# GpSimd's maximum over partitions: `partition_all_reduce` against the stock `tensor_reduce` into one partition

## Chip, cores, metric

One core of one Trainium2 chip. The metric is the device time of one execution in microseconds (us). The profile is of one execution; its span is shorter than the reported time (164.46 against 162.6 for the kernel before).

## The reference

```python
def setup_inputs():
    batch, seq, dim = 32, 512, 1024
    return {"x": np.random.randn(batch, seq, dim).astype(np.float32)}

def reference(x):
    return np.max(x, axis=-1).astype(np.float32)
```

This is 16,384 rows of 1024 f32, 67.1 MB in, one maximum per row out. A block of 128 rows is one row per partition, so there are 128 blocks.

## The kernel before

The rows are loaded into a ring of 46 blocks, and VectorE takes the row maxima (`reduce` below). Five of the 128 blocks, all from loads near the end, go by a side road, so that VectorE has less to do there. On it TensorE turns a block, after which a row's 1024 values lie over 128 partitions and 8 chunks; ScalarE copies it out of PSUM; GpSimd takes the maximum over the partitions; TensorE turns the one row of answers back; VectorE merges the 8 chunks.

```python
TENSOR = {                      # after which load which block is turned or turned back
    8: [("turn", 8, 0), ("back", 8, 0)],
    9: [("turn", 9, 0), ("turn", 9, 1), ("turn", 9, 2), ("back", 9, 0)],
    12: [("turn", 12, 0), ("back", 9, 1), ("back", 9, 2), ("back", 12, 0)],
}
BY_GPSIMD = {8: 1, 9: 3, 12: 1} # blocks of each load that take the side road
MERGE = {9: 8, 15: 9, 18: 12}   # after which load VectorE merges whose blocks
# ... cut ...
    turned = ctx.enter_context(tc.tile_pool(name="turned", bufs=2))
    allr = ctx.enter_context(tc.tile_pool(name="allr", bufs=2))
# ... cut ...
    def turn(j, k):
        rows, cols = tiles[j]
        ps = psum.tile([P, D], F32)
        for c in range(C):
            in_turn("PE", nc.tensor.transpose(out=ps[:, c * P:(c + 1) * P],
                in_=rows[:, k, c * P:(c + 1) * P], identity=ident))
        sb = turned.tile([P, D], F32)
        nc.scalar.copy(out=sb, in_=ps)
        top = allr.tile([P, D], F32)
        nc.gpsimd.partition_all_reduce(top, sb, P, bass_isa.ReduceOp.max)
        tops[j, k] = top

    def back(j, k):
        # ... cut ...
        for c in range(C):
            in_turn("PE", nc.tensor.transpose(out=backs[j][:, k, c:c + 1],
                in_=tops[j, k][0:1, c * P:(c + 1) * P], identity=ident[0:1, 0:1]))
# ... cut: for each load
            reduce = in_turn("DVE", nc.vector.reduce_max(
                out=cols[:, :n - m], in_=xc[:, :n - m, :], axis=X))
            if j in MERGE:
                i = MERGE[j]
                in_turn("DVE", nc.vector.reduce_max(out=tiles[i][1], in_=backs[i], axis=X))
```

VectorE and TensorE run in program order. A merge that isn't ready therefore stops VectorE.

## Time and profile before

| | before |
|---|---|
| time | 164.46 us (2 runs, 164.42 to 164.5) |
| VectorE busy | 135.0 us, 83% of the span |
| GpSimd busy | 16.3 us, 10% |
| loads' share of the DMA engines | 96.6% |

Two things are nearly full, VectorE at the end and the DMA engines throughout. GpSimd is idle for its first 134 us.

### The profile page before, as it was taken

What the parts mean: (1) busy time and instruction counts of PE and PEld (TensorE: products, weight loads), DVE (VectorE), ACT (ScalarE), POOL (GpSimd) and SP (SyncE); (2) the same over time, 40 slices, a digit from 0 to 9 for tenths busy, and PEclk for the clock granted to TensorE, in tenths of its full rate; (3) what the DMA queues carried; (4) which work ended last, traced back from release to release, by engine and by line L of the source; (5) the groups of instructions that cost most, each with busy time, mean ns of one, the idle gap of its engine ahead of it and who ended that gap; (6) DMA issues with size and microseconds to landing.
All of it is one profiled execution on the core that took longest, in us unless ns stands there. A gap on an engine that the chain in (4) does not pass through costs nothing.

```text
span 162.6 us, 293 instructions
## 1 busy us (share of the span) xinstructions
PE 13.0 (8%) x80; PEld 11.7 (7%) x80; DVE 135.0 (83%) x33; ACT 6.3 (4%) x6; POOL 16.3 (10%) x9
## 2 busy tenths in 40 slices
PE   0000000000000000000000000000000040943520
PEld 0000000000000000000000000000000030933420
DVE  3000079995999779999996999999999999999994
ACT  3000000000000000000000000000000011240200
POOL 0000000000000000000000000000000007099910
PEclk9999999999999999999999999999999999985555
DMA  7999699988999799999998989999999999999990
GB/s 242 484 484 438 287 484 484 484 378 348 484 484 484 333 498 432 445 419 419 419 419 387 499 388 427 417 426 408 417 435 435 471 399 426 423 418 409 406 368 16
DMA packets 3456, 67.18 MB, mean 413 GB/s; under 512 B 640, under 2 KB 640, under 8 KB 1792
## 3 DMA queue, kind: packets, MB, share of 16 engines
q1 hardware_dynamic: 3168, 67.11, 96.6%
q10 hardware_dynamic: 288, 0.07, 0.2%
HBM read 67.11 MB, written 0.07 MB: 413 GB/s over the span
## 4 chain that ended last, share of the span: by engine, by line
DVE 54%; DMA 44%; SPq 0%; issue 0%
DVE res L139 53%; DMA ring<-in_x_dram 44%; DVE res L156 0%; DVE tail L155 0%; SPq L133 0%; DVE res L143 0%
## 5 line engine op out<-in xcount | busy, mean ns | idle before, releaser
L139 DVE TENSOR_REDUCE res<-ring 128x1 f32<-128x1024 f32 (+6 forms) x20 | 132.1, 6653 | 24.3 <-DMA ring<-in_x_dram 24.3
L106 POOL PARTITION_ALL_REDUCE top<-sb x5 | 16.1, 3255 | 138.8 <-ACT sb L104 138.8
L98 PE MATMUL ps<-ident,ring 128*128 128x128 f32 x40 | 8.1, 382 | 134.2 <-DMA ring<-in_x_dram 131.8
L98 PEld LDWEIGHTS ps<-ident,ring 128*128 128x128 f32 x40 | 7.1, 204 | 134.3 <-issue 134.2
L104 ACT COPY sb<-ps 128x1024 f32<-128x1024 f32 x5 | 5.1, 1013 | 144.9 <-PE ps L98 143.0
L115 PE MATMUL fetched<-ident,top 1*128 1x1 f32 x40 | 5.0, 243 | 9.1 <-POOL top L106 9.1
L115 PEld LDWEIGHTS fetched<-ident,top 1*128 1x128 f32 x40 | 4.6, 214 | 10.3 <-POOL top L106 9.8
L104 ACT ACT_TABLE_LOAD x1 | 1.3, 1283 | 0.7 <-PEq L176 0.7
L76 DVE MEMSET ident<- 128x128 f32 x1 | 0.2, 165 | 0.8 <-PEq L176 0.8
L156 DVE TENSOR_REDUCE res<-tail 128x1 f32<-128x513 f32 x1 | 0.7, 686 | 0.0
L155 DVE TENSOR_REDUCE tail<-ring 128x1 f32<-128x512 f32 x1 | 0.7, 675 | 0.0
L83 DVE TENSOR_SCALAR rowno<-rowno 32x1 f32<-32x1 f32 x3 | 0.4, 147 | 0.1
L143 DVE TENSOR_REDUCE res<-fetched 128x1 f32<-128x8 f32 (+1 forms) x3 | 0.5, 161 | 0.0
L78 DVE TENSOR_TENSOR_SCAN colno<-ident 128x128 f32<-128x128 f32 x1 | 0.4, 425 | 0.0
L85 DVE TENSOR_SCALAR ident<-colno,rowno 128x128 f32<-128x128 f32 x1 | 0.3, 287 | 0.0
L80 DVE STREAM_TRANSPOSE rowno<-colno 128x32 f32<-128x32 f32 x1 | 0.2, 211 | 0.0
L176 POOL MEMSET const-float32-0.0<- 128x1 f32 x1 | 0.1, 99 | 0.2 <-issue 0.2
L176 POOL MEMSET const-uint8-127<- 128x1 uint8 x1 | 0.1, 103 | 0.0
L176 POOL MEMSET const-bfloat16-1.0<- 128x1 bf16 x1 | 0.1, 102 | 0.0
L176 POOL MEMSET const-float32-1.0<- 128x1 f32 x1 | 0.1, 99 | 0.0
L77 DVE MEMSET rowno<- 128x32 f32 x1 | 0.1, 85 | 0.0
## 6 DMA issues: line engine op xcount, KB each, us to landing
ring<-in_x_dram SPq DMA_DIRECT2D x3, 7680.0 KB, 38.4
ring<-in_x_dram SPq DMA_DIRECT2D x2, 6656.0 KB, 34.6
ring<-in_x_dram SPq DMA_DIRECT2D x2, 4608.0 KB, 37.8
ring<-in_x_dram SPq DMA_DIRECT2D x2, 3072.0 KB, 31.9
ring<-in_x_dram SPq DMA_DIRECT2D x1, 5632.0 KB, 28.6
ring<-in_x_dram SPq DMA_DIRECT2D x7, 512.0 KB, 22.3
ring<-in_x_dram SPq DMA_DIRECT2D x2, 1536.0 KB, 34.9
ring<-in_x_dram SPq DMA_DIRECT2D x1, 1024.0 KB, 33.4
```

The costliest lines, as they stand in the source:

```text
L78: in_turn("DVE", nc.vector.tensor_tensor_scan(out=colno, data0=ident, data1=ident, initial=-1.0, op0=ALU.add, op1=ALU.mult))
L83: in_turn("DVE", nc.vector.tensor_scalar(out=part, in0=part, scalar1=float(q * 32), scalar2=None, op0=ALU.add))
L85: in_turn("DVE", nc.vector.tensor_scalar(out=ident, in0=colno, scalar1=rowno[:, 0:1], scalar2=None, op0=ALU.is_equal))
L98: in_turn("PE", nc.tensor.transpose(out=ps[:, c * P:(c + 1) * P], in_=rows[:, k, c * P:(c + 1) * P], identity=ident,))
L104: nc.scalar.copy(out=sb, in_=ps)
L106: nc.gpsimd.partition_all_reduce(top, sb, P, bass_isa.ReduceOp.max)
L115: in_turn("PE", nc.tensor.transpose(out=backs[j][:, k, c:c + 1], in_=tops[j, k][0:1, c * P:(c + 1) * P], identity=ident[0:1, 0:1],))
L139: reduce = in_turn("DVE", nc.vector.reduce_max(out=cols[:, :n - m], in_=xc[:, :n - m, :], axis=X))
L143: in_turn("DVE", nc.vector.reduce_max(out=tiles[i][1], in_=backs[i], axis=X))
L155: in_turn("DVE", nc.vector.reduce_max(out=tail[:, PAD - 1:PAD], in_=half, axis=X))
L156: in_turn("DVE", nc.vector.reduce_max(out=res[:, I - 1:], in_=tail[:, PAD - 1:], axis=X))
L176: nc = _bacc.Bacc("TRN2", target_bir_lowering=False, num_devices=1)
```

## The change

The intent is to use the stock instruction: a `tensor_reduce` over the partition axis needs no special routine and writes one partition, which is all that `back` reads, where `partition_all_reduce` writes the answer to all 128.

```diff
-from concourse import bass_isa, bass_utils, mybir
+from concourse import bass_utils, mybir
@@
-        top = allr.tile([P, D], F32)
-        nc.gpsimd.partition_all_reduce(top, sb, P, bass_isa.ReduceOp.max)
+        top = allr.tile([1, D], F32)
+        nc.gpsimd.tensor_reduce(out=top, in_=sb, axis=mybir.AxisListType.C, op=ALU.max)
```

## The prediction

> **What bounds the kernel now.** I read the chain of work that ended last first, because only what lies on it can move the end.
>
> ```profile
> DVE 54%; DMA 44%; SPq 0%; issue 0%
> DVE res L139 53%; DMA ring<-in_x_dram 44%; DVE res L156 0%; DVE tail L155 0%; SPq L133 0%; DVE res L143 0%
> ```
>
> GpSimd (POOL) is not on it. The span of 162.6 us is loads followed by VectorE's row maxima (L139), and at the end VectorE alone. Then the groups of instructions, for what GpSimd does and how long each takes:
>
> ```profile
> L139 DVE TENSOR_REDUCE res<-ring 128x1 f32<-128x1024 f32 (+6 forms) x20 | 132.1, 6653 | 24.3 <-DMA ring<-in_x_dram 24.3
> L106 POOL PARTITION_ALL_REDUCE top<-sb x5 | 16.1, 3255 | 138.8 <-ACT sb L104 138.8
> L104 ACT COPY sb<-ps 128x1024 f32<-128x1024 f32 x5 | 5.1, 1013 | 144.9 <-PE ps L98 143.0
> L115 PE MATMUL fetched<-ident,top 1*128 1x1 f32 x40 | 5.0, 243 | 9.1 <-POOL top L106 9.1
> L143 DVE TENSOR_REDUCE res<-fetched 128x1 f32<-128x8 f32 (+1 forms) x3 | 0.5, 161 | 0.0
> ```
>
> Five blocks of 128 rows leave VectorE: TensorE turns each (L98), ScalarE copies it out (L104), GpSimd takes the maximum over the 128 partitions in 3.255 us (L106), TensorE turns the answer back from partition 0 (L115), and VectorE merges it (L143). The last column of L143 is an idle time of 0.0: VectorE never waits for this side road. Its slack comes from the timeline near the end, whose columns are start, length, engine and operation:
>
> ```profile
> 133.73 1.01 ACT L104 COPY sb<-ps 128x1024 f32<-128x1024 f32 x1 [131.73 <-PE ps L98]
> 134.84 3.23 POOL L106 PARTITION_ALL_REDUCE top<-sb  x1 [134.41 <-ACT sb L104]
> 138.11 1.01 PE L115 MATMUL fetched<-ident,top 1*128 1x1 f32 x8 [4.42 <-POOL top L106]
> 142.17 9.64 POOL L106 PARTITION_ALL_REDUCE top<-sb  x3 [4.11 <-ACT sb L104]
> 142.93 0.15 DVE L143 TENSOR_REDUCE res<-fetched 128x1 f32<-128x8 f32 x1
> 150.80 2.07 PE L115 MATMUL fetched<-ident,top 1*128 1x1 f32 x16
> 152.06 3.23 POOL L106 PARTITION_ALL_REDUCE top<-sb  x1 [0.26 <-ACT sb L104]
> 154.13 0.17 DVE L143 TENSOR_REDUCE res<-fetched 128x3 f32<-128x24 f32 x1
> 155.34 1.01 PE L115 MATMUL fetched<-ident,top 1*128 1x1 f32 x8 [2.48 <-POOL top L106]
> 157.69 0.15 DVE L143 TENSOR_REDUCE res<-fetched 128x1 f32<-128x8 f32 x1
> 160.39 0.34 ACTq L161 DMA_DIRECT2D out_dram<-res  x1
> ```
>
> The turned answers are there at 139.12, 152.87 and 156.35; VectorE takes them at 142.93, 154.13 and 157.69. The slacks are 3.8, 1.3 and 1.3 us. Four reductions end before the second merge, so about 1.3 / 4 = 0.3 us more per reduction is free. Beyond that GpSimd sets the end.
>
> **What the Trainium skill says.** GPSIMD Engine Reference, section "3.2 Cross-partition — where GPSIMD wins": "Measured at [128, 2048]: `tensor_reduce` along the partition axis takes 247,699 ns." Neither operation nor type is given. The trace of the kernel before has no such instruction; it shows the other way to the same result at 3.255 us for 128x1024. The same page, section "2.1 Instruction dispatch", gives a first call to a freshly loaded GpSimd kernel about 6 us that no profile instruction shows. This trace disagrees for the instruction it has: the first of the five starts 0.1 us after its input and takes 3.23 us, like the others. Perfetto Trace Analysis, section "GPSIMD Engine Instruction", calls GpSimd spans unreliable and advises start-to-start spacing; here they agree, three in a row taking 9.64 us, 3.21 each.
>
> **The change, part by part.** The instruction order shows the same rows on PE, VectorE, ScalarE and the load queue; on GpSimd five PARTITION_ALL_REDUCE give way to five TensorReduce into one partition, with the same waits.
>
> *Removed:* 5 x 3.255 = 16.3 us of GpSimd, all beside VectorE's work, and the writing of 127 partitions that nobody reads. Worth nothing by itself.
>
> *Added:* five partition-axis reductions of 1024 columns. Taking the page's figure as proportional to the columns, one is 247.70 / 2 = 123.85 us (an estimate from that page), 38 times the present one. That is 121 ns per column against 3.2 ns now. It may look absurd, but the new instruction is the stock one, the old one a routine made for this purpose, and the page measured the stock one on this engine. Nothing measured speaks for another figure, so I take it.
>
> *On the path.* With T for one reduction:
> 1. The first starts at 134.84, as now: nothing before it changes.
> 2. Between its end and the second's start lie 4.10 us (138.07 to 142.17): turning back 1.01, turning the next block, the copy of 1.01. This gap stays, because TensorE's order puts the back turn of the first block ahead of the three turns of the next.
> 3. The other four run end to end. Their inputs must be ready: two copies fit in the two buffers, and each further copy needs only the reduction two earlier to end. For the fifth, its load and turn (now the cause of the 0.26 us wait) fall under 124 us of reductions. Five in all: 5 x 123.85 = 619.3 us.
> 4. After the last one: 0.05 to the back turn, 1.01 for it, 0.1 to VectorE, then what now lies between the start of the last merge and the end of the span, 162.6 - 157.69 = 4.91 (a row maximum, the two half rows, the store). Sum 6.07.
> 5. The span: 134.84 + 4.10 + 619.25 + 6.07 = 764.3 us. The reported time lies 164.46 - 162.6 = 1.86 over the span: 766.1 us.
>
> In general the time is 146.9 + 5T once T is over the slack. *Moved:* VectorE keeps its 135.0 us of busy time but stands at each of the three merges. Merge one comes at 134.84 + 123.85 + 1.2 = 259.9 instead of 142.93 (a wait of some 117 us). Merge two comes after four reductions, 134.84 + 4.10 + 495.4 + 1.2 = 635.5; VectorE has done what lies between by about 271, so some 364 us of wait. Merge three at 759.4, with VectorE ready at 639.2: some 120 us. VectorE frees ring slots late, so the last loads issue late as well; once VectorE resumes they need about 10 to 40 us (the DMA issues land in 9 to 38 us), which lies under the next reduction. No further cost.
>
> **The rivals.**
> *A: as fast as now, or faster* (T at most 3.5 us). One output partition instead of 128 is less writing, and the present 3.255 us proves that the engine can do the job at this rate. Then VectorE and the loads bound as before: 164.5 us. There is no gain, since GpSimd's present time is off the chain and even T = 0 takes no wait from VectorE. Against it is a measured figure 38 times larger. I give it 3%.
> *B: slow, but cheaper than the figure.* The page names neither the operation nor the type. If a maximum of f32 costs half of what was timed there, T is 62 and the time 457; at two thirds, T is 82.6 and the time 560. This is the main uncertainty, and it points down. I give T under 110 us about 25%.
> *C: a fixed part in the figure.* If part of the 247.7 us doesn't depend on the columns, T is above 123.85; wholly fixed would give T = 247.7 and 1385 us. A load of 6 us on the first call would add 6, making 772. A large fixed part is unlikely for work that goes through the columns; I give T over 130 us some 8%.
> *D: VectorE or the loads hold GpSimd back.* Block 12's load waits for ring slots that VectorE frees only after merge one. If that load landed after the third reduction it would add a gap. Some 25 to 40 us against more than 200 us of reductions make this improbable at any T over 15 us.
>
> **Range and chances.** The middle is the proportional figure, 766 us. The upper edge is T = 130.6 (5% fixed part or first-call cost): 800. The lower edge is T = 66.6, where the maximum is only a little over half of what the page timed: 480. The range is wide below because of rival B, and leaves about 1 in 10 on each side. Slower by over 2% needs only T over about 4 us, hence 0.96. Within 2% is rival A at 0.03. Faster needs a wait that GpSimd now causes on the chain, and none is there: 0.01.
>
> **What would show it.** In the changed kernel's profile: five reductions on L106 of about 123,850 ns and POOL busy about 619 us, 81% of the span; the chain that ended last mostly POOL top L106, in place of VectorE and DMA; L143 with about 600 us of idle time released by PE, in three waits in the ratio 1 : 3 : 1; the same busy time on DVE (135.0), PE and ACT; the DMA mean falling to about 67.18 MB / 764 us = 88 GB/s. A start of the first reduction at 134.8 proves step 1, a gap of 4.1 us after it step 2, no other gap on POOL step 3, and 6 us from the last reduction to the end step 4. The prediction is wrong if L106 shows another mean; the formula is then still tested by 146.9 + 5T. It is wrong in mechanism if the time leaves that formula by over 3 us, that is if reductions don't run end to end.

## The result

The changed kernel takes 458.86 us (2 runs, 458.82 to 458.89). The ratio of fast runs is 2.79 (95% interval 2.786 to 2.797). A ratio is the mean time of one kernel's fast runs over that of the other's of the same rounds, so not quite the ratio of the medians quoted.

The groups of instructions of the changed kernel; columns as before: busy us, mean ns of one, then the idle time before them and who ended it.

```profile
L106 POOL CROSS_LANE_REDUCE top<-sb 128x1024 f32<-128x1024 f32 x5 | 312.3, 62478 | 138.4 <-ACT sb L104 138.4
L139 DVE TENSOR_REDUCE res<-ring 128x1 f32<-128x1024 f32 (+6 forms) x20 | 131.9, 6651 | 24.3 <-DMA ring<-in_x_dram 24.3
L143 DVE TENSOR_REDUCE res<-fetched 128x1 f32<-128x8 f32 (+1 forms) x3 | 0.5, 172 | 294.5 <-PE fetched L115 294.5
L115 PE MATMUL fetched<-ident,top 1*128 1x1 f32 x40 | 5.0, 243 | 306.3 <-POOL top L106 306.3
```

The reduction went from 3.255 to 62.478 us. VectorE's work is as it was (131.9 against 132.1 us on L139, with the same 24.3 us of waits for loads), but its merges on L143, which waited 0.0 us before, now wait 294.5 us. That is the whole difference of the spans: 457.1 - 162.6 = 294.5 us.

The timeline of the changed kernel, cut to the reductions and the merges (what lies between the lines is left out):

```profile
134.76 62.54 POOL L106 CROSS_LANE_REDUCE top<-sb 128x1024 f32<-128x1024 f32 x1 [134.31 <-ACT sb L104]
198.40 0.17 DVE L143 TENSOR_REDUCE res<-fetched 128x1 f32<-128x8 f32 x1 [55.45 <-PE fetched L115]
201.38 249.76 POOL L106 CROSS_LANE_REDUCE top<-sb 128x1024 f32<-128x1024 f32 x4 [4.08 <-ACT sb L104]
389.83 0.18 DVE L143 TENSOR_REDUCE res<-fetched 128x3 f32<-128x24 f32 x1 [180.24 <-PE fetched L115]
452.24 0.17 DVE L143 TENSOR_REDUCE res<-fetched 128x1 f32<-128x8 f32 x1 [58.85 <-PE fetched L115]
```

The first reduction starts at the same moment as before (134.76 against 134.84). After one gap of 4.08 us the other four run end to end (249.76 / 4 = 62.44 us each), to 451.14. VectorE stops three times, and the end follows 5.96 us after the last reduction.

The chain of work that ended last needs care here:

```profile
POOL 28%; POOLq 27%; DMA 22%; issue 14%; DVE 7%; PE 1%; ACT 0%; SPq 0%
```

GpSimd's own share seems to be only 28%. The rest of its time is under POOLq and "issue": one POOLq piece runs from 327.50 to 451.15, where the timeline has the last two reductions back to back. In the kept trace this piece is a DRAIN of the program's end (L187), recorded from 327.50 on for 123.70 us, beside those reductions. The chain is inferred from semaphore events and followed that record instead. The three shares together, 69%, are the 68% of the span for which GpSimd is busy. The timeline decides, not the chain.

So the form of the prediction, 146.9 + 5T, held: with the measured T it gives 146.9 + 312.3 = 459.2 us for 458.86 measured. What failed is T, 62.5 us against the predicted 123.85. The experiments ask why.

### The profile page after: what moved, and what is told of

The parts are those of the page before. It is cut to its first block, busy times and chain, and to the rows that moved or that the text cites. A ratio compares the mean times of both kernels' runs of the same rounds, so it can differ in the third digit from the quotient of the medians.

```text
span 457.1 us, 293 instructions
## 1 busy us (share of the span) xinstructions
PE 14.2 (3%) x80; PEld 12.7 (3%) x80; DVE 135.1 (30%) x33; ACT 6.3 (1%) x6; POOL 312.5 (68%) x9
## 4 chain that ended last, share of the span: by engine, by line
POOL 28%; POOLq 27%; DMA 22%; issue 14%; DVE 7%; PE 1%; ACT 0%; SPq 0%
POOL top L106 28%; POOLq L187 27%; DMA ring<-in_x_dram 22%; DVE res L139 7%; PE ps L98 1%; ACT sb L104 0%; PE fetched L115 0%; DVE res L156 0%; DVE tail L155 0%; SPq L133 0%; DVE res L143 0%
## 5 line engine op out<-in xcount | busy, mean ns | idle before, releaser
L106 POOL CROSS_LANE_REDUCE top<-sb 128x1024 f32<-128x1024 f32 x5 | 312.3, 62478 | 138.4 <-ACT sb L104 138.4
L139 DVE TENSOR_REDUCE res<-ring 128x1 f32<-128x1024 f32 (+6 forms) x20 | 131.9, 6651 | 24.3 <-DMA ring<-in_x_dram 24.3
L143 DVE TENSOR_REDUCE res<-fetched 128x1 f32<-128x8 f32 (+1 forms) x3 | 0.5, 172 | 294.5 <-PE fetched L115 294.5
L98 PE MATMUL ps<-ident,ring 128*128 128x128 f32 x40 | 9.3, 425 | 131.7 <-DMA ring<-in_x_dram 131.7
L98 PEld LDWEIGHTS ps<-ident,ring 128*128 128x128 f32 x40 | 8.1, 227 | 131.7 <-issue 131.7
```

Of the source, the lines that this page charges most:

```text
L106: nc.gpsimd.tensor_reduce(out=top, in_=sb, axis=mybir.AxisListType.C, op=ALU.max)
L139: reduce = in_turn("DVE", nc.vector.reduce_max(out=cols[:, :n - m], in_=xc[:, :n - m, :], axis=X))
```

## The experiments

The theory formed on this result is that the page's figure belongs to another operation than a maximum. The rivals: it belongs to another type; the cost isn't proportional to the columns, so that half of 2048 columns isn't half of the time; or the figure isn't met on this chip at all.

### Five sums in place of five maxima (wrong result)

```diff
-        nc.gpsimd.tensor_reduce(out=top, in_=sb, axis=mybir.AxisListType.C, op=ALU.max)
+        nc.gpsimd.tensor_reduce(out=top, in_=sb, axis=mybir.AxisListType.C, op=ALU.add)
```

> All five reductions add instead of taking the maximum (wrong result on purpose, same shapes and types). If the page's figure was for a sum and the maximum is the cheaper operation, one reduction takes about 123.9 us and the run 146.9 + 5 x 123.9 = 766 us. If the operation makes no difference, one takes 62.5 us and the run 459 us. In both cases the sum 146.9 + 5T should hold within 3 us.

Measured: 712.69 us (one run; 164.3 for the kernel before on the same chip). The five reductions in the view of the tile `top` (least, median and most ns of one, then the first and the last start):

```profile
L106 POOL CROSS_LANE_REDUCE top<-sb x5: 113211/113211/113306, 134.7 to 591.7; 128x1024 f32<-128x1024 f32 x5
```

The operation makes most of the difference: a sum costs 113.2 us, 1.81 times a maximum. It isn't quite the 123.9 us expected. The formula holds: 146.9 + 5 x 113.2 = 712.9.

### The cost by number of columns

The changed kernel with six reductions of a constant tile ahead, in GpSimd's idle time. The probe tiles take their turn in the buffers of `turned` and `allr`, so that they need no memory of their own.

```diff
+    probe = turned.tile([P, D], F32, tag="sb")
+    answer = allr.tile([1, D], F32, tag="top")
+    in_turn("DVE", nc.vector.memset(probe, 2.0))
+    # ... cut: one line each for n = 32, 64, 128, 256, 512, 1024; the five reductions of turn() are put in turn behind them
+    in_turn("POOL", nc.gpsimd.tensor_reduce(out=answer[:, :n], in_=probe[:, :n], axis=mybir.AxisListType.C, op=ALU.max))
```

> The changed kernel, with six more maxima over partitions of a constant tile put into GpSimd's idle first 134 us: 32, 64, 128, 256, 512 and 1024 columns. If the cost is proportional to the columns (61 ns each): 2.0, 3.9, 7.8, 15.6, 31.2 and 62.4 us, in all 123 us, so the run stays at 459 us. If there is a large fixed part or the cost grows faster than the columns, the ratios of neighbours leave 2. If the first call pays for loading, the 32-column one is about 6 us too long, or starts late. If the cost depends on the data, the 1024-column one on a constant differs from the 62.4 us on the real data.

Measured: 458.83 us, result correct. The timeline on GpSimd:

```profile
3.68 2.19 POOL L91 CROSS_LANE_REDUCE answer<-probe 128x32 f32<-128x32 f32 x1 [3.23 <-DVE probe L90]
5.94 4.13 POOL L92 CROSS_LANE_REDUCE answer<-probe 128x64 f32<-128x64 f32 x1
10.14 8.03 POOL L93 CROSS_LANE_REDUCE answer<-probe 128x128 f32<-128x128 f32 x1
18.24 15.81 POOL L94 CROSS_LANE_REDUCE answer<-probe 128x256 f32<-128x256 f32 x1
34.12 31.39 POOL L95 CROSS_LANE_REDUCE answer<-probe 128x512 f32<-128x512 f32 x1
65.58 62.53 POOL L96 CROSS_LANE_REDUCE answer<-probe 128x1024 f32<-128x1024 f32 x1
```

The cost is proportional: (62.53 - 31.39) / 512 = 60.8 ns per column, and a fixed part of 2.19 - 32 x 0.0608 = 0.24 us. A constant tile takes as long as the real data. The first one isn't longer than its size says, and it starts 0.1 us after its input. The rivals of a fixed part, of a cost that grows faster than the columns and of a cost that depends on the data fall.

### Operation, type, partitions, and both axes

```diff
+    # ... cut: the tiles probe (f32), narrow (bf16) and answer, both inputs filled with 2.0
+    # 256 columns each: max f32, add f32, max bf16, add bf16, max f32 over 32 partitions, max over all axes
+    in_turn("POOL", nc.gpsimd.tensor_reduce(out=answer[:, :256], in_=probe[:, :256], axis=mybir.AxisListType.C, op=ALU.max))
+    in_turn("POOL", nc.gpsimd.tensor_reduce(out=answer[:, :256], in_=probe[:, :256], axis=mybir.AxisListType.C, op=ALU.add))
+    in_turn("POOL", nc.gpsimd.tensor_reduce(out=answer[:, :256], in_=narrow[:, :256], axis=mybir.AxisListType.C, op=ALU.max))
+    in_turn("POOL", nc.gpsimd.tensor_reduce(out=answer[:, :256], in_=narrow[:, :256], axis=mybir.AxisListType.C, op=ALU.add))
+    in_turn("POOL", nc.gpsimd.tensor_reduce(out=answer[:, :256], in_=probe[:32, :256], axis=mybir.AxisListType.C, op=ALU.max))
+    in_turn("POOL", nc.gpsimd.tensor_reduce(out=answer[:, :1], in_=probe[:, :256], axis=mybir.AxisListType.XYZWC, op=ALU.max))
```

> The changed kernel, with six more reductions of 256 columns in GpSimd's idle first part: max of f32, sum of f32, max of bf16, sum of bf16, max of f32 over 32 partitions only, and max over partitions and columns together (one number out). The first should take 15.6 us. Theory operation: both sums take 31 us, both maxima 15.6. Theory type: bf16 takes 31 us whatever the operation. If the work is done for all lanes whatever their number, 32 partitions cost 15.6 us; if partition by partition, 3.9. If what costs is the step across the lanes, once for each column, the last one takes 1 us or so; if it is the reading, 15.6. In all under 134 us, so the run stays at 459 us.

Measured: 458.96 us, correct. The timeline on GpSimd, in the order of the diff:

```profile
3.67 15.82 POOL L93 CROSS_LANE_REDUCE answer<-probe 128x256 f32<-128x256 f32 x1 [3.23 <-DVE probe L91]
19.56 28.50 POOL L94 CROSS_LANE_REDUCE answer<-probe 128x256 f32<-128x256 f32 x1
48.14 15.82 POOL L95 CROSS_LANE_REDUCE answer<-narrow 128x256 f32<-128x256 bf16 x1
64.03 28.51 POOL L96 CROSS_LANE_REDUCE answer<-narrow 128x256 f32<-128x256 bf16 x1
92.61 15.76 POOL L97 CROSS_LANE_REDUCE answer<-probe 32x256 f32<-32x256 f32 x1
108.43 0.75 POOL L98 CROSS_LANE_REDUCE answer<-probe 128x1 f32<-128x256 f32 x1
```

The operation counts (15.82 against 28.50 us), the input type doesn't (f32 and bf16 agree within 0.01 us): the rival of the type falls. A quarter of the partitions costs the same. The last line reads the same 256 columns but gives one number instead of 256, and takes 0.75 us. If it reads and folds the columns as the others do, this is at most 0.75 / 256 = 2.9 ns of the 60.8 ns per column, and nearly all the time goes with the number of results. That fits a step across the lanes made once for each result, as expected, but no run separates this step from, say, the writing of a result. The "correct" of the runs with added reductions is that of the kernel's own output; what the added reductions gave wasn't checked, only timed.

### The page's own size

```diff
-    allr = ctx.enter_context(tc.tile_pool(name="allr", bufs=2))
+    allr = ctx.enter_context(tc.tile_pool(name="allr", bufs=1))
+    # ... cut: probe is [128, 1024], filled with 2.0; twice reads it two times over, answers is [1, 2, 1024]
+    in_turn("POOL", nc.gpsimd.tensor_reduce(out=answers, in_=twice, axis=mybir.AxisListType.C, op=ALU.max))
+    in_turn("POOL", nc.gpsimd.tensor_reduce(out=answers, in_=twice, axis=mybir.AxisListType.C, op=ALU.add))
```

> The changed kernel, with two reductions of 2048 columns (the page's size) ahead of the five: a maximum, then a sum. Proportional: the maximum 124.9 us. The sum: 247.7 us if the page's figure is a sum of f32; 124.9 if the operation makes no difference, and then the page's figure is not met here; 247.7 for both if the cost grows faster than the columns above 1024. The run's time is pushed back by what goes beyond GpSimd's idle 134 us (some 240 us if the sum takes 247.7), and is of no interest; one buffer for the results instead of two, to make room.

Measured: 683.1 us, correct. The timeline on GpSimd:

```profile
3.67 124.83 POOL L93 CROSS_LANE_REDUCE answer<-sb 128x2048 f32<-128x2048 f32 x1 [3.23 <-DVE sb L90]
128.57 226.37 POOL L94 CROSS_LANE_REDUCE answer<-sb 128x2048 f32<-128x2048 f32 x1
```

At 2048 columns (1024 columns read twice over, not a tile of 2048) the maximum takes 124.8 us and the sum 226.4. The skill's 247.7 us (GPSIMD Engine Reference, section "3.2 Cross-partition — where GPSIMD wins") is 1.98 times the maximum and 1.09 times the sum. It is near a sum and far from a maximum, but nothing run here meets it exactly. That the page timed a sum is therefore likely but not shown, and why the last 9% are missing stays open.

### The other instruction by the same yardstick

The kernel before with six `partition_all_reduce` of a constant tile in GpSimd's idle time (64 to 1024 columns as maxima, then 1024 as a sum).

```diff
+    in_turn("POOL", nc.gpsimd.partition_all_reduce(answer[:, :n], probe[:, :n], P, bass_isa.ReduceOp.max))
```

> The kernel before, with six more partition_all_reduce in GpSimd's idle first part: maxima of 64, 128, 256, 512, 1024 columns, then a sum of 1024. The maximum of 1024 should take 3.2 us. If it is 3.1 ns per column with little fixed part, 512 takes 1.6 and 64 some 0.2; a fixed part shows as a floor. The sum takes 3.2 us if here the operation makes no difference, 6.4 if a sum costs double here as well. Time 164.5 us.

Measured: 164.47 us, correct. The timeline on GpSimd:

```profile
3.67 0.52 POOL L91 PARTITION_ALL_REDUCE answer<-probe  x1 [3.25 <-DVE probe L90]
...
6.23 1.78 POOL L94 PARTITION_ALL_REDUCE answer<-probe  x1
8.11 3.22 POOL L95 PARTITION_ALL_REDUCE answer<-probe  x1
11.42 6.11 POOL L96 PARTITION_ALL_REDUCE answer<-probe  x1
```

Here a column costs (3.22 - 1.78) / 512 = 2.8 ns, with 0.34 us fixed, though the answer is written to all 128 partitions. The number of partitions written is therefore not what makes the stock one slow. Per column it is 60.8 / 2.8 = 22 times dearer. A sum is also dearer in this instruction (6.11 us, 1.9 times).

### Only the first, or only the last, by the stock instruction

Two kernels made from the kernel before, with j == 8 (first) or j == 12 (last):

```diff
+        if j == 8:
+            top = allr.tile([1, D], F32)
+            nc.gpsimd.tensor_reduce(out=top, in_=sb, axis=mybir.AxisListType.C, op=ALU.max)
+        else:
             top = allr.tile([P, D], F32)
             nc.gpsimd.partition_all_reduce(top, sb, P, bass_isa.ReduceOp.max)
```

> The kernel before, with only the first of the five blocks reduced by the stock tensor_reduce; the other four by partition_all_reduce. With T = 62.44 once and 3.23 four times the prediction's sum gives 146.9 + 62.4 + 12.9 = 222.2 us (a few tenths more if the fifth still waits for its turn). [...]the program has a switch between them that neither of the two kernels has in mid-run: if a switch costs about 6 us it shows as a GpSimd gap between the first and second reduction above the 4.1 us of the other kernels, and the run is at 226 or more (the 4.1 us of the round trip may hide most of it).

> The kernel before, with only the last block reduced by the stock tensor_reduce. It starts at 152.06 as before, and 62.44 us later plus 6.07 + 1.86 us of what follows: 222.4 us. So the place of the slow one among the five makes no difference. If the switch of libraries costs, the reduction starts later by that much less the 0.26 us that GpSimd waits there anyway, and the run ends as much later.

Measured: 224.21 us with the first, 231.49 us with the last, both correct. One stock reduction is enough to cost about 60 us, as the first of the five or as the last. The excess over the sum, 2.0 and 9.1 us, is at the switch from one instruction to the other. GpSimd's timeline, first kernel:

```profile
134.91 62.54 POOL L107 CROSS_LANE_REDUCE top<-sb 128x1024 f32<-128x1024 f32 x1 [134.48 <-ACT sb L104]
203.33 12.88 POOL L110 PARTITION_ALL_REDUCE top<-sb  x4 [5.87 <-ACT sb L104]
```

and the second:

```profile
142.27 9.63 POOL L110 PARTITION_ALL_REDUCE top<-sb  x3 [4.11 <-ACT sb L104]
161.21 62.53 POOL L107 CROSS_LANE_REDUCE top<-sb 128x1024 f32<-128x1024 f32 x1 [9.31 <-issue]
```

The gap is 5.87 us where it is 4.1 without a switch, and 9.31 us where it is 0.26. No view prints what fills it, but the kept traces record it: two records named MODIFY_POOL_CONFIG (POOL is GpSimd) right at the end of the last reduction of the old kind, at 197.67 and 197.71 us in the first kernel, at 151.85 and 151.89 us in the second. The kernels before and after have only two, at 0.75 to 0.83 us, and the kernel without the side road (below) has none. In the first kernel the round trip hides most of the switch; in the second nothing does. I expected about 6 us for both directions. Towards the stock instruction it was 9.3. Towards the other it was at most 5.9, and not surely all of that: its first reduction also starts 0.1 us after ScalarE's second copy ends (203.23).

### No side road at all

```diff
-TENSOR = { ... }
-BY_GPSIMD = {8: 1, 9: 3, 12: 1}
-MERGE = {9: 8, 15: 9, 18: 12}
+TENSOR = {}
+BY_GPSIMD = {}
+MERGE = {}
```

> The kernel before without the side road: VectorE takes all 128 blocks itself. Five more rows at 16.16 / 15 = 1.08 us each are 5.4 us, less three merges of 0.1 us: VectorE never waits after 89 us, so all of it should be on the path: 169.5 us. If so, a stock reduction of 62.4 us must never be on the path for more than a row's worth of 1.08 us, and the changed kernel is best repaired by giving GpSimd nothing. If the loads are the bound in the last stretch (96.6% busy), less: 165 to 167 us.

Measured: 169.16 us (4 runs), ratio 1.030 to the kernel before (1.028 to 1.031); correct. The side road is worth 4.8 us in the kernel before. A stock reduction on the path costs 62 us to save VectorE a block of 1.08 us.

### One stock reduction, begun early

If only the slack decides, a slow reduction may be hidden by starting it at 92 us.

```diff
 TENSOR = {
-    8: [("turn", 8, 0), ("back", 8, 0)],
-    9: [("turn", 9, 0), ("turn", 9, 1), ("turn", 9, 2), ("back", 9, 0)],
-    12: [("turn", 12, 0), ("back", 9, 1), ("back", 9, 2), ("back", 12, 0)],
+    4: [("turn", 4, 0)],
+    18: [("back", 4, 0)],
 }
-BY_GPSIMD = {8: 1, 9: 3, 12: 1}
+BY_GPSIMD = {4: 1}
-MERGE = {9: 8, 15: 9, 18: 12}
+MERGE = {18: 4}
```

> The changed kernel with one block instead of five on the side road, and that block taken from the fifth load, which lands at 89 us, the last point at which VectorE still waits for a load. The stock reduction then runs from 92.3 to 154.8 us, the back turn ends at 155.9, and VectorE merges it after the load that it handles at about 160: no wait. If the cost on the path is only what ends after the slack, one row less than in the kernel without the side road, 1.08 less 0.1 for the merge: 169.16 - 1.0 = 168.2 us. If a 62 us reduction costs something else (a wait of the merge, a hold on the ring), 169.2 or more.

> The kernel without the side road once more, on the same chip as the early block, for the difference of about 1 us: 169.2 us.

Measured: 169.09 us (4 runs) and 169.15 us (5 runs), ratios 1.0290 and 1.0292 to the kernel before. The reduction is hidden, as expected, but the gain of 1.0 us isn't there. The timeline of the early one:

```profile
92.38 62.54 POOL L105 CROSS_LANE_REDUCE top<-sb 128x1024 f32<-128x1024 f32 x1 [91.93 <-ACT sb L103]
102.53 21.55 DVE L138 TENSOR_REDUCE res<-ring 128x11 f32<-128x11264 f32 x2 [0.37 <-DMA ring<-in_x_dram]
124.37 38.14 DVE L138 TENSOR_REDUCE res<-ring 128x9 f32<-128x9216 f32 x12 [0.29 <-DMA ring<-in_x_dram]
...
162.43 0.15 DVE L142 TENSOR_REDUCE res<-fetched 128x1 f32<-128x8 f32 x1
```

The merge waits for nothing: 62.5 us on GpSimd cost nothing when begun 70 us ahead. VectorE isn't slowed meanwhile either (9.75 us for nine blocks, against 9.74). But VectorE, with a block less to do by 102 us, now waits for two loads (0.37 + 0.29 = 0.66 us; all its waits for loads are 24.9 us against 24.2 without the side road), and the merge takes its 0.1. Of its lead over the kernel without the side road, 0.54 us at the first of these loads (102.53 against 103.07), 0.16 us is left at the second (124.37 against 124.53). A block taken from VectorE there is given back to the loads. No kernel tried beats the kernel before.

## Why the prediction was right or wrong

- *GpSimd is off the path now, with a slack of some 0.3 us per reduction:* fits; the merges' 0.0 us of wait became 294.5. The limit itself wasn't tried between 3.2 and 62 us.
- *Step 1, the first reduction starts at 134.84:* right, 134.76. *Step 2, one gap of 4.10 us:* right, 4.08. *Step 3, no other gap:* right, four in 249.76 us. *Step 4, 6.07 us after the last:* right, 5.96. *The sum, 146.9 + 5T:* right within 0.5 us at T = 62.5 and at T = 113.2.
- *T = 123.85 us:* wrong, and with it the time. This is the step that failed, the term *Added*: the mechanism was right, and five reductions were counted at 123.85 us that measured 62.48 us each. That is 306.9 us too much, which is the whole of 766 - 459. Halving the skill's figure for half the columns was sound (60.8 ns per column from 32 to 1024, and 124.83 us at 2048). Taking the figure over for a maximum was not: a maximum of the page's size takes 124.83 us here and not 247.7, and a sum takes 1.81 times as long as a maximum. "Nothing measured speaks for another figure" was no evidence for this one, since the page named no operation.
- *Rival B* named the likely cause and nearly the number ("T is 62 and the time 457"); T under 110 us got 25%. The range ended at T = 66.6, just above that; with a figure of unnamed operation it should have reached below half of it.
- *Rival C:* a fixed part exists and is 0.24 us. No first-call cost appears in the changed kernel. That the trace of the kernel before "disagrees" with the page on this was read too strongly: its first reduction came 134 us after its MODIFY_POOL_CONFIG, which would hide 6 us. A cost does appear when a program changes from one instruction to the other: GpSimd gaps of 5.87 and 9.31 us where 4.1 and 0.26 were without the change.
- *Rival A* fell: T is 62.5 us, not 3.5 or less. *Rival D* fell too: no load held GpSimd back, and VectorE's waits for loads stayed at 24.3 us. The reading behind it, that late merges make the last loads issue late, was wrong, without effect on the time: they issue at 148.81 and 150.08 us, before the first merge at 198.40, where the kernel before has 148.85 and 150.13. (The "9 to 38 us" of landing are medians of groups; the longest single load took 56.1 us.)
- *The waits in the ratio 1 : 3 : 1, about 600 us:* 55.5, 180.2 and 58.9, together 294.5 us; the ratio right, the size wrong with T. *The chain mostly POOL:* the view gave it only 28% by name, for the reason shown.

## What to carry to other kernels

Before a helper engine's instruction is swapped, compare its new duration with the slack at the point where the result is consumed: here some 0.3 us (an estimate from the timeline) was free for each of five, and every microsecond beyond came back five times (712.69 - 458.86 us for 113.2 - 62.5 us more), because VectorE runs in order here and stands at the merge. A duration from a table is worth only as much as its label; if it doesn't name the operation, put one instruction of the right operation into an idle stretch of the same engine and measure it, which here cost nothing in time. And look at how many results the stock reduction over partitions gives: here it was cheap for one number (0.75 us from 128x256) and dear for a row of them (62 us for 1024).

## What the Trainium skill lacked or had wrong

- GPSIMD Engine Reference, section "3.2 Cross-partition — where GPSIMD wins": its 247,699 ns at [128, 2048] names no operation or type. Here a maximum took 124.8 us and a sum 226.4 us; type makes no difference (15.82 us for f32 and bf16 at 256 columns). The figure was met by neither, the sum being 9% below it.
- The same section gives one size and so no rule. The runs show 60.8 ns per column for a maximum plus 0.24 us, whatever the number of partitions (15.76 us for 32, 15.82 for 128), and 0.75 us when the columns are reduced as well.
- No page of the skill names `partition_all_reduce`, let alone its price: here 2.8 ns per column plus 0.34 us for a maximum, 6.11 us for a sum of 1024 columns. GPSIMD Engine Reference, section "4.1 Engine selection", says to use GpSimd for a reduction over partitions without saying that its two ways differ by 22 times per column.
- The same page, section "2.1 Instruction dispatch", has about 6 us for the first call to a freshly loaded kernel. With only one of the two instructions in the program none of it shows: in the run with six sizes the first reduction starts at 3.68 us, 2.9 us after the MODIFY_POOL_CONFIG and 0.1 us after its input, and isn't too long (why, no run shows). A switch in mid-program left GpSimd gaps of up to 5.9 us towards `partition_all_reduce` and 9.3 us towards the stock instruction; the page has no figure by direction.
